# A two-model decoder kernel: retention, dilated and memory keys and the PLE rows turned by VectorE and a trip over DRAM

## The chip, the cores and the metric

The kernel is one program on one core of a Trainium2 chip. The metric is device time in microseconds (us) of one launch; lower is better. Of the kernel before, three runs are shown. Beside them stands one profiled execution, from which all durations of single instructions, waits and transfers are taken. Engine names are those of the profile: PE is TensorE's matmul stream, PEld its weight loads, DVE VectorE, ACT ScalarE, POOL GpSimd, SP the SyncE queue that issues all DMAs.

## The reference

Two stacks run one after the other on the same 256 x 1024 activations. Everything is float32.

```
first_block, 2 layers:
  mix   = hybrid_mixer(x)              # convolution + sparse attention + chunk attention, then w_mix_out
  x     = layer_norm(ALPHA*x + mix)
  k, v  = split(mem @ w_mkv)           # 256 memory rows, 4 heads of 256  -> "memory keys"
  cross = softmax(q k^T / 16) v @ w_mo ;  x = layer_norm(ALPHA*x + cross)
  x     = layer_norm(ALPHA*x + relu(x @ w1)^2 @ w2)
second_block, 4 layers (i = 0..3):
  a = rmsnorm(h)
  i = 0, 3: retention                  # q, k roped, 4 heads of 256; (q k^T * decay) v; silu(g) * y @ w_out
  i = 1   : dilated attention          # 3 groups x 16 heads of 64, windows 128/512/2048, dilations 1/4/16
  i = 2   : gated MLP with a token mix
  h = h + rmsnorm(mix) ;  h = h + rmsnorm(swiglu(rmsnorm(h)))
  emb  = p[i] @ ple_w_proj[i]          # 256 rows of 256: the "PLE rows"
  h    = h + sigmoid(rmsnorm(h) @ ple_w_gate[i]) * emb
```

## The kernel before

The 256 rows are two tiles of 128, and each tile t is worked by a Python generator, `thread(t)`. All weights form one list of blocks, mostly 128 x 1024 elements (512 KB), in the order of use. For each block n the main loop issues the loads up to `LOAD_AHEAD` = 6 blocks ahead (`load`, L199), splits the next block into a high and a low part (`split`: high on ACT at L225 or L284, low on DVE at L228 or L232), then lets thread 0 use block n and thread 1 use block n - lag, where the lag is 1 to 5 by stage (`LAGS`; 4 for the retention's "rq" and "rk", 1 for "dq", "dk", "dv", 5 for "pg"). Loaded blocks have 5 raw buffers, split parts 14. The order in which each engine gets its instructions is then set at build time by a scheduler over this program.

Each projection (`proj`) takes four blocks. Per block and thread it issues six 128x512 matmuls (high x high, high x low, low x high for two slices of the contraction, L326) into one of two banks "pj", which both threads share, and then calls `flush(t)`. `flush` runs what was put off: closures in `later[t]`, entries of `due[t]` that are counted down by one at each flush, and one step of a generator in `behind[t]` (attention that runs beside the projections).

A matmul contracts over partitions, so queries, keys and hidden rows have to be turned before they are used. There are two ways to do that in the kernel:

- `transpose4` (L279): up to four 128x128 blocks pass through TensorE against the identity matrix into one PSUM bank, and ACT or DVE copies the bank to SBUF. Retention queries and keys ("rqp", copied by ACT at L920), dilated queries and keys ("dqp", "dkp", copied by DVE at L1044), memory keys ("mkp", copied by DVE at L815) and PLE rows ("prp", cut by ACT at L284 and DVE at L315) go this way.
- `turn_by_dma`: DVE transposes 32x32 squares of the row block into a tile "xt" (L360, one instruction), four DMAs write it to a DRAM tile "xd" (L364, 64 KB each), one DMA reads it back turned into the source's own buffer (L367, `BACK` = 1 flush later), and `CUT` = 3 flushes later ACT and DVE cut it into high and low parts (L378, L379). Only the hidden rows of the feed-forward, retention and gated-MLP outputs go this way. "xt" comes from two buffers tagged "ET", which both threads share with the turned softmax rows of the attention.

The stages in order of time, by rows of the trace: the first block's last hidden row is squared at 850 us (L375); retention i = 0 copies its first query at 865 us (L905); the dilated scores run from 1313 to 1570 us (L979); the gated MLP's outputs are turned from 1872 to 1936 us (L360); the second retention copies its last key at 2228 us (L920); the last PLE rows are turned at 2566 us. The end of each layer of the second block is `embedding`: it loads the PLE rows, turns and cuts them and multiplies them with two blocks ("pep"), between the norm and the gate projection of the same thread.

Of the kernel before, what the change touches and what calls it, by code (L numbers as in the profile page):

```python
# [8 lines left out]
F32 = mybir.dt.float32  # L9
# [6 lines left out]
P = 128  # L16
# [14 lines left out]
DEFER = (1, 1, 1, 1, 1, 1, 1, 1)  # L31
# [17 lines left out]
def kernel(  # L49
# [7 lines left out]
    nc = tc.nc  # L57
# [294 lines left out]
        else:  # L352
            fn()

    def turn_by_dma(t, src, nkk, parts, j, square=None):


        w = 32 * nkk
        xt = sb.tile([P, 512], F32, tag=ETB[0].format(t=t), name="xt", bufs=ETB[1])[:, :4 * w]
        V.transpose(xt.rearrange("p (q k a) -> p q k a", q=4, a=32), src.rearrange("p (k q a) -> p q k a", q=4, a=32))  # L360
        d_ = dr.tile([4, 32, 4, P], F32, tag=f"xd{t}", name="xd")
        dv = d_.rearrange("q a i e -> (q a i e)")[0:P * 4 * w].rearrange("(q a i e) -> q a i e", q=4, a=32, i=4)
        for i in range(4):
            nc.sync.dma_start(dv[:, :, i, :].rearrange("q a e -> a q e"),  # L364
                              xt[32 * i:32 * i + 32, :].rearrange("a (q e) -> a q e", q=4))
        z = src
        due[t].append([BACK, lambda: nc.sync.dma_start(z, dv.rearrange("q a i e -> (q a) (i e)"))])  # L367

        def fin():
            bank = parts.banks[j] = newbank(t)  # L370
            zv = z.rearrange("p (i k b) -> p k i b", i=4, k=nkk)
            hi, lo = (x[:, 0:nkk, :].rearrange("p k (i b) -> p k i b", i=4) for x in bank)
            if square:
                f = sb.tile([P, 4, P], F32, tag=f"tq{t}", name="ffT", bufs=2)
                S.activation(f[:, 0:nkk, :].rearrange("p k (i b) -> p k i b", i=4), zv, AF.Square, scale=square)  # L375
                cut(bank, slice(0, nkk), f[:, 0:nkk, :])
            else:
                S.copy(hi, zv)  # L378
                V.tensor_tensor(out=lo, in0=zv, in1=hi.bitcast(F32), op=ALU.subtract)  # L379

        due[t].append([CUT, fin])
        due[t].sort(key=lambda d: d[0])

    def proj(t, xT, key, n, kind="pj"):
        p = bank(kind, t, [P, 512], "pj")
# [418 lines left out]
    def memory_block(t, l, j):  # L804

        own = slice(t * P, (t + 1) * P)
        p = yield from proj(t, memT[t], ("mkv", l, j), 512)
        if j < 2:
            r_ = sb.tile([P, 512], F32, tag=f"rB{t}", name="mk", bufs=2)
            S.copy(r_, p)  # L810
            kT = get2(("mkT", l, j), [P, 4, 256], "kv", 4)

            def turn():
                pt = transpose4(t, [r_[:, i * P:(i + 1) * P] for i in range(4)], "mkp")
                V.tensor_copy(kT[:, :, own], pt)  # L815

            defer(t, DEFER[7], turn)
        else:
            vv = get2(("mv", l, t), [P, D], "kv", 4)
            S.copy(vv[:, 512 * (j - 2):512 * (j - 1)], p)  # L820
# [6 lines left out]
    def cross(t, l, xT):  # L827
        qT = []
        oT = Parts()
        for j in range(2):  # L830
            p = yield from proj(t, xT, ("mq", l, j), 512)
            q = sb.tile([P, 512], F32, tag=f"rA{t}", name="mqr", bufs=2)
            if j:
                V.tensor_scalar(out=q, in0=p, scalar1=0.0625, scalar2=None, op0=ALU.mult)
            else:
                S.mul(q, p, 0.0625)
            pt = transpose4(t, [q[:, i * P:(i + 1) * P] for i in range(4)], "mqp")
            qT.append(sb.tile([P, 4, P], F32, tag=f"tq{t}", name="mqT", bufs=2))
            copy("s" if j else "v", qT[j], pt)
        for b in range(2):  # L840
            kT = shared[("mkT", l, b)]
            sp = bank("at", t, [P, 2, 256], "msp")
            for i in range(2):
                for c in range(2):
                    T.matmul(sp[:, i, :], qT[b][:, 2 * i + c, :], kT[:, 2 * i + c, :],
                             start=(c == 0), stop=(c == 1))
            pt, et, ev = turn_bank(t, softmax_bank(t, sp, 2, 2), 2)
            copy("v", et, pt)
            o = pt
            for i in range(2):  # L850
                for c in range(2):
                    c0 = 512 * b + 256 * i + 128 * c
                    for kt in range(2):
                        T.matmul(o[:, 2 * i + c, :], shared[("mv", l, kt)][:, c0:c0 + P], ev[:, i, kt, :],
                                 start=(kt == 0), stop=(kt == 1))
            oT.banks.append(newbank(t))
            cut(oT.banks[b], slice(0, 4), o, IALPHA)
        acc = newacc(t)
        yield from outproj(t, acc, ("mo", l), 8, oT, 0, True, True, xT)
        return acc  # L860
# [21 lines left out]
    def retention(t, i, hT, rs):  # L882
# [11 lines left out]
        hr = scaled(t, rs, 0.5, "hr")  # L894
        cbx = rcos[:, t:t + 1, :].to_broadcast([P, 4, P])
        sbx = rsin[:, t:t + 1, :].to_broadcast([P, 4, P])
        qT = [sb.tile([P, 4, P], F32, tag=f"tq{t}", name="rqT", bufs=2) for _ in range(2)]
        for nm in ("rq", "rk"):
            for j in range(2):
                p = yield from proj(t, hT, (nm, i, j), 512)  # L900
# [12 lines left out]
                bv = b.rearrange("p (h c) f -> p h c f", c=2)  # L913
                V.tensor_tensor(out=xv[:, :, 0, :], in0=xv[:, :, 0, :], in1=bv[:, :, 1, :], op=ALU.subtract)
                V.tensor_tensor(out=xv[:, :, 1, :], in0=xv[:, :, 1, :], in1=bv[:, :, 0, :], op=ALU.add)
                dst = qT[j] if nm == "rq" else get2(("rkT", i, j), [P, 4, 256], "kv", 4)[:, :, own]

                def turn(xs=xs, dst=dst):
                    pt = transpose4(t, [xs[:, k, :] for k in range(4)], "rqp")
                    S.copy(dst, pt)  # L920

                defer(t, DEFER[4], turn)
        acc = newacc(t)
        oT = Parts()
        for h in range(5):
            if h < 4:
# [6 lines left out]
                for c in range(nt):  # L933
                    kt = t - c
                    for d in range(2):
                        T.matmul(sp[:, c, :], kT[:, 2 * (h % 2) + d, kt * P:(kt + 1) * P], qT[h // 2][:, 2 * (h % 2) + d, :],  # L936
                                 start=(d == 0), stop=(d == 1))
                sm_ = sb.tile([P, 2, P], F32, tag=f"sc{t}", name="rsm")
                V.tensor_tensor(out=sm_[:, 0, :], in0=sp[:, 0, :], in1=rmask[:, h, :], op=ALU.mult)
                if t:  # L940
# [23 lines left out]
    def dilated(t, hT, rs):  # L964
# [6 lines left out]
        def attend(BT, qT, kT, vv, us, mx, sm_):  # L971
            firsts = [0, 1] if t == 0 else [0, 1, 4, 5]
            for b0 in range(0, len(firsts), 2):
                sps = [bank("at", t, [P, 512], "dsp").rearrange("p (h k) -> p h k", h=hpb) for _ in range(2)]
                for i in range(hpb):
                    for b in range(2):
                        h = firsts[b0 + b] + 2 * i
                        r = 64 * (h % 2)
                        T.matmul(sps[b][:, i, :], qT[r:r + 64, h // 2, :], kT[r:r + 64, h // 2, :nk],  # L979
                                 start=True, stop=True)  # L980
                sls = [slice(h0, h0 + 2 * hpb - 1, 2) for h0 in firsts[b0:b0 + 2]]
                es = []
                for b in range(2):
# [48 lines left out]
        for hf in range(2):  # L1032
# [3 lines left out]
            for g in range(3):  # L1036
                p = yield from proj(t, hT, ("dq", hf, g), 512)
                r_ = sb.tile([P, 512], F32, tag=f"rA{t}", name="dqr", bufs=2)
                S.activation(r_, p, AF.Copy, scale=sq[:, 0:1])
                qT = sb.tile([P, 4, P], F32, tag=f"tq{t}", name="ddqT", bufs=2)  # L1040

                def turn(r_=r_, dst=qT, nm="dqp"):
                    pt = transpose4(t, [r_[:, k * P:(k + 1) * P] for k in range(4)], nm)
                    V.tensor_copy(dst, pt)  # L1044

                defer(t, DEFER[5], turn)
                p = yield from proj(t, hT, ("dk", hf, g), 512)
                r_ = sb.tile([P, 512], F32, tag=f"rB{t}", name="dkr", bufs=2)
                S.activation(r_, p, AF.Copy, scale=rs[:, 0:1])
                kT = get2(("ddkT", hf, g), [P, 4, 256], "kv", 4)  # L1050
                defer(t, DEFER[5], lambda r_=r_, dst=kT[:, :, own], turn=turn: turn(r_, dst, "dkp"))
                p = yield from proj(t, hT, ("dv", hf, g), 512)
                vv = get2(("ddv", hf, g), [P, 2, 512], "kv", 4)
                S.activation(vv[:, t, :], p, AF.Copy, scale=rs[:, 0:1])
                us = sb.tile([P, 8, 64], F32, tag=f"U{t}", name="dUs", bufs=3)
                U.append(us)
                behind[t].append(attend(tiles[("db", hf, g)], qT, kT, vv, us, mall[:, g, :], sall[:, g, :]))
# [62 lines left out]
    def swiglu(t, i, hT, rs):  # L1120
# [2 lines left out]
        V.tensor_tensor(out=sc, in0=rs, in1=hr, op=ALU.mult)  # L1123
        acc = newacc(t)
        fT = Parts()
        for j in range(7):
            if j < 6:
                n = FG[j][1]
                nkk = n // P
# [11 lines left out]
        return acc  # L1141

    def embedding(t, i):
        pr = sb.tile([P, 256], F32, tag=f"sc{t}", name="pr")
        nc.sync.dma_start(pr, p2[i, t * P:(t + 1) * P, :])
        pt = transpose4(t, [pr[:, 0:P], pr[:, P:2 * P]], "prp")
        pT = Parts()
        pT.banks.append(newbank(t))
        cut(pT.banks[0], slice(0, 2), pt[:, 0:2, :])
        pp = [bank("pj", t, [P, 512], "pep") for _ in range(2)]  # L1150
        yield from outproj(t, pp, ("pp", i), 2, pT, 0, True, True)
        e = []
# [176 lines left out]
```

## Time and profile before

| what | value |
|---|---|
| runs | 2593.28, 2594.84, 2595.04 us; median 2594.84 us |
| profiled execution | 2594.81 us, span 2593.1 us, mean granted clock 0.998 |
| busy, share of the span | PE 98%, PEld 80%, DVE 70%, ACT 58%, POOL 2% |
| DMA | 500.97 MB, mean 193 GB/s, 62.7% of 16 engines on the SP queue |
| HBM | read 471.33 MB, written 27.26 MB |

The span runs from the first to the last instruction of the profiled execution; its time has 1.7 us more. A busy share is the share of the span in which an engine had an instruction running. Matmuls are pipelined, so the cost of one in a dense stream is read from the distance between starts in the timeline, not from its duration (a 128x512 matmul lasts 390 to 400 ns and starts every 0.23 us).

### The profile page before, as it was taken

To read this page: it belongs to the slowest core of one execution; us is meant where nothing else is said; L and a number is where in the kernel's file an instruction comes from. 1 tells how busy PE (TensorE), PEld (TensorE's weight loads), DVE (VectorE), ACT (ScalarE), POOL (GpSimd) and SP (SyncE) were. 2 spreads that over 40 slices of the span, in tenths; PEclk is the share of its full clock that TensorE was granted. 3 is DMA by queue.
4 is the path that set the end of the run, shared out by engine and by line. 5 is a ranking of instruction groups with operands and counts; after the bars stand their busy time and mean duration, and the time that the engine had idled before them with its cause. 6 is when DMAs were issued, how large, how long until landed. Compare 5 with 4: busy or idle time off the path is not lost. (4 is left out here: it accounts for less than half of the span.)

```text
span 2593.1 us, 36098 instructions
## 1 busy us (share of the span) xinstructions
PE 2546.9 (98%) x12308; PEld 2079.4 (80%) x12308; DVE 1815.5 (70%) x3333; ACT 1509.7 (58%) x2852; POOL 58.6 (2%) x88
## 2 busy tenths in 40 slices
PE   8999999999999999999999999999999999999998
PEld 7788788887788778788787878887877887887887
DVE  8865667866666866766766767667867677766766
ACT  6653555654455665555766666557656566655555
POOL 0000000000000000000000000000100000000000
PEclk9999999999999999999999999999999999999999
DMA  6453776554578566676654555766586775666764
GB/s 214 157 171 106 224 241 188 155 175 143 170 233 243 175 201 218 206 226 211 211 161 142 162 162 159 228 204 215 166 263 208 220 226 177 198 205 190 230 201 146
DMA packets 280904, 500.97 MB, mean 193 GB/s; under 512 B 28816, under 2 KB 101648, under 8 KB 279568
## 3 DMA queue, kind: packets, MB, share of 16 engines
q1 hardware_dynamic: 280720, 498.68, 62.7%
q8 instruction: 96, 1.57, 0.3%
q14 instruction: 88, 0.72, 0.1%
HBM read 471.33 MB, written 27.26 MB: 192 GB/s over the span
## 5 line engine op out<-in xcount | busy, mean ns | idle before, releaser
L326 PE MATMUL pj<-wh,part 128*128 128x512 f32 (+3 forms) x4480 | 1426.6, 385 | 2.5 <-ACT part L284 1.4
L326 PEld LDWEIGHTS pj<-wh,part 128*128 128x128 f32 x4480 | 832.3, 188 | 168.0 <-issue 9.4
L326 PE MATMUL pj<-wl,part 128*128 128x512 f32 (+3 forms) x2240 | 853.1, 381 | 1.3 <-DVE wl L228 1.3
L326 PE MATMUL acc<-wh,part 128*128 128x512 f32 x1920 | 582.7, 396 | 13.1 <-ACT part L284 6.3
L326 PEld LDWEIGHTS pj<-wl,part 128*128 128x128 f32 x2240 | 422.5, 189 | 77.0 <-issue 2.6
L326 PEld LDWEIGHTS acc<-wh,part 128*128 128x128 f32 x1920 | 358.0, 189 | 93.1 <-ACT part L284 8.4
L326 PE MATMUL acc<-wl,part 128*128 128x512 f32 x960 | 308.5, 394 | 0.1
L232 DVE TENSOR_TENSOR wl<-ff,wh 128x512 fp32r<-128x512 f32 x256 | 169.8, 686 | 104.2 <-ACT wh L284 104.2
L284 ACT CAST wh<-ff 128x512 fp32r<-128x512 f32 x256 | 152.8, 620 | 134.6 <-PE acc L326 65.3
L326 PEld LDWEIGHTS acc<-wl,part 128*128 128x128 f32 x960 | 181.5, 189 | 38.6 <-DVE wl L232 0.4
L225 ACT ACTIVATE wh<-fg,ngc 128x512 fp32r<-128x512 f32 (+1 forms) x192 | 126.5, 686 | 120.6 <-PE pj L326 64.1
L228 DVE SCALAR_TENSOR_TENSOR wl<-fg,ngc,wh 128x512 fp32r<-128x512 f32 (+1 forms) x192 | 129.5, 701 | 80.5 <-ACT wh L225 80.4
L228 DVE SCALAR_TENSOR_TENSOR wl<-fu,ngc,wh 128x512 fp32r<-128x512 f32 (+1 forms) x192 | 128.1, 704 | 51.8 <-ACT wh L225 48.6
L225 ACT ACTIVATE wh<-fu,ngc 128x512 fp32r<-128x512 f32 (+1 forms) x192 | 123.8, 684 | 59.8 <-PE acc L326 35.7
L284 ACT CAST wh<-fo 128x512 fp32r<-128x512 f32 x176 | 103.6, 621 | 78.0 <-PE pj L326 76.4
L232 DVE TENSOR_TENSOR wl<-fo,wh 128x512 fp32r<-128x512 f32 x176 | 115.0, 684 | 44.7 <-ACT wh L284 41.9
L225 ACT ACTIVATE wh<-rv,ngc 128x512 fp32r<-128x512 f32 x64 | 45.2, 722 | 40.9 <-PE pj L326 33.6
L232 DVE TENSOR_TENSOR wl<-ro,wh 128x512 fp32r<-128x512 f32 x64 | 43.4, 688 | 29.3 <-ACT wh L284 29.3
L228 DVE SCALAR_TENSOR_TENSOR wl<-rv,ngc,wh 128x512 fp32r<-128x512 f32 x64 | 46.8, 747 | 24.5 <-ACT wh L225 24.3
L228 DVE SCALAR_TENSOR_TENSOR wl<-pg,ngc,wh 128x512 fp32r<-128x512 f32 x64 | 46.5, 747 | 20.6 <-ACT wh L225 20.1
L232 DVE TENSOR_TENSOR wl<-mkv,wh 128x512 fp32r<-128x512 f32 x64 | 41.9, 686 | 26.7 <-ACT wh L284 26.5
L284 ACT CAST wh<-ro 128x512 fp32r<-128x512 f32 x64 | 39.3, 620 | 36.1 <-PE pj L326 28.6
(323 smaller groups left out, 3214.1 us busy)
## 6 DMA issues: line engine op xcount, KB each, us to landing
ff<-in_w_ff_dram SPq DMA_DIRECT2D x128, 512.0 KB, 4.3
fo<-in_ffn_out_dram SPq DMA_DIRECT2D x88, 512.0 KB, 4.4
fg<-in_ffn_in_dram SPq DMA_DIRECT2D x80, 512.0 KB, 4.5
fu<-in_ffn_in_dram SPq DMA_DIRECT2D x80, 512.0 KB, 4.1
xd<-xt SPq DMA_DIRECT2D x384, 64.0 KB, 2.4
mkv<-in_w_mkv_dram SPq DMA_DIRECT2D x32, 512.0 KB, 4.0
rv<-in_ret_in_dram SPq DMA_DIRECT2D x32, 512.0 KB, 4.5
rg<-in_ret_in_dram SPq DMA_DIRECT2D x32, 512.0 KB, 3.8
```

What stands on the lines that cost most here:

```text
L225: S.activation(h_, r_, AF.Copy, scale=gc)
L228: V.scalar_tensor_tensor(out=l_, in0=r_, scalar=gc, in1=h_.bitcast(F32), op0=ALU.mult, op1=ALU.subtract)
L232: (V if le == "v" else G).tensor_tensor(out=l_, in0=r_, in1=h_.bitcast(F32), op=ALU.subtract)
L284: S.copy(o, i)
L326: T.matmul(outs[i], a, ws[i][b], start=s0, stop=s1)
```

## The change

Four kinds of rows leave `transpose4`. Two helpers are cut out of `turn_by_dma`: `trip` (the 32x32 transposes and the four DMAs out) and `put_off` (an entry in `due`). A new helper `turn_to` uses them. If the destination can take the order in which the rows come back, the DMA writes straight into it; otherwise the DMA comes back into the source and ACT copies from there with the columns put in order.

The key tiles, and the retention's query tile, get an order of columns with 32 tokens of one feature slice in a row, so that DMA can write them: memory keys `[P, 8, 4, 32]`, dilated keys `[P, 8, 4, 32]`, retention queries `[P, 4, 4, 32]`. The score matmuls read them as 8 or 4 runs of 32 elements. Retention keys (`[P, 2, 4, P]`) and dilated queries keep whole columns and take the copy on ACT. The PLE rows are loaded at step j = 3 of the feed-forward, sent on the trip at j = 4 and cut 21 flushes later; `embedding` only picks them up.

```
+    def trip(t, src, nkk):
         w = 32 * nkk
...      # xt, V.transpose, xd and the four DMAs out as before
+        return dv.rearrange("q a i e -> (q a) (i e)")
+
+    def put_off(t, n, f):
+        due[t].append([n, f])
+        due[t].sort(key=lambda d: d[0])
+
+    def turn_to(t, src, nkk, dst):
+        back = trip(t, src, nkk)
+        if len(dst.shape) == 3:
+            put_off(t, BACK, lambda: nc.sync.dma_start(src, back))
+            put_off(t, CUT, lambda: S.copy(dst.rearrange("p k (i b) -> p k i b", b=32),
+                                           src.rearrange("p (i k b) -> p k i b", i=4, b=32)))
+        else:
+            put_off(t, BACK, lambda: nc.sync.dma_start(dst.rearrange("p i k b -> p (i k b)"), back))
+
+    def turn_by_dma(t, src, nkk, parts, j, square=None, at=CUT):
+        back = trip(t, src, nkk)
         z = src
+        put_off(t, BACK, lambda: nc.sync.dma_start(z, back))
...
+        put_off(t, at, fin)
...  memory_block
-            kT = get2(("mkT", l, j), [P, 4, 256], "kv", 4)
-            def turn():
-                pt = transpose4(t, [r_[:, i * P:(i + 1) * P] for i in range(4)], "mkp")
-                V.tensor_copy(kT[:, :, own], pt)
-            defer(t, DEFER[7], turn)
+            kT = get2(("mkT", l, j), [P, 8, 4, 32], "kv", 4)
+            turn_to(t, r_, 4, kT[:, 4 * t:4 * t + 4])
...  cross
-                    T.matmul(sp[:, i, :], qT[b][:, 2 * i + c, :], kT[:, 2 * i + c, :],
+                    T.matmul(sp[:, i, :].rearrange("p (i b) -> p i b", b=32), qT[b][:, 2 * i + c, :], kT[:, :, 2 * i + c, :],
...  retention
-        qT = [sb.tile([P, 4, P], F32, tag=f"tq{t}", name="rqT", bufs=2) for _ in range(2)]
+        qT = [sb.tile([P, 4, 4, 32], F32, tag=f"tq{t}", name="rqT", bufs=2) for _ in range(2)]
...
-                dst = qT[j] if nm == "rq" else get2(("rkT", i, j), [P, 4, 256], "kv", 4)[:, :, own]
-                def turn(xs=xs, dst=dst):
-                    pt = transpose4(t, [xs[:, k, :] for k in range(4)], "rqp")
-                    S.copy(dst, pt)
-                defer(t, DEFER[4], turn)
+                turn_to(t, xf, 4, qT[j] if nm == "rq" else get2(("rkT", i, j), [P, 2, 4, P], "kv", 4)[:, t])
...
-                        T.matmul(sp[:, c, :], kT[:, 2 * (h % 2) + d, kt * P:(kt + 1) * P], qT[h // 2][:, 2 * (h % 2) + d, :],
-                                 start=(d == 0), stop=(d == 1))
+                        f = 2 * (h % 2) + d
+                        T.matmul(sp[:, c, :].rearrange("p (i b) -> p i b", b=32), kT[:, kt, f, :],
+                                 qT[h // 2][:, :, f, :], start=(d == 0), stop=(d == 1))
...  dilated
-                        T.matmul(sps[b][:, i, :], qT[r:r + 64, h // 2, :], kT[r:r + 64, h // 2, :nk],
-                                 start=True, stop=True)
+                        T.matmul(sps[b][:, i, :].rearrange("p (i b) -> p i b", b=32), qT[r:r + 64, h // 2, :],
+                                 kT[r:r + 64, 0:4 * nkt, h // 2, :], start=True, stop=True)
...
-                def turn(r_=r_, dst=qT, nm="dqp"):
-                    pt = transpose4(t, [r_[:, k * P:(k + 1) * P] for k in range(4)], nm)
-                    V.tensor_copy(dst, pt)
-                defer(t, DEFER[5], turn)
+                turn_to(t, r_, 4, qT)
...
-                kT = get2(("ddkT", hf, g), [P, 4, 256], "kv", 4)
-                defer(t, DEFER[5], lambda r_=r_, dst=kT[:, :, own], turn=turn: turn(r_, dst, "dkp"))
+                kT = get2(("ddkT", hf, g), [P, 8, 4, 32], "kv", 4)
+                turn_to(t, r_, 4, kT[:, 4 * t:4 * t + 4])
...  swiglu
+        pT = shared[("pT", i, t)] = Parts()
+        pT.banks.append(None)
         for j in range(7):
+            if j == 3:
+                pr = sb.tile([P, 256], F32, tag=f"sc{t}", name="pr")
+                nc.sync.dma_start(pr, p2[i, t * P:(t + 1) * P, :])
+            if j == 4:
+                turn_by_dma(t, pr, 2, pT, 0, at=21)
...  embedding
-        pr = sb.tile([P, 256], F32, tag=f"sc{t}", name="pr")
-        nc.sync.dma_start(pr, p2[i, t * P:(t + 1) * P, :])
-        pt = transpose4(t, [pr[:, 0:P], pr[:, P:2 * P]], "prp")
-        pT = Parts()
-        pT.banks.append(newbank(t))
-        cut(pT.banks[0], slice(0, 2), pt[:, 0:2, :])
+        pT = shared.pop(("pT", i, t))
```

More of the change, by code (lines that the diff above doesn't have):

```diff
@@ L353, in defer @@
             fn()
-    def turn_by_dma(t, src, nkk, parts, j, square=None):
+    def trip(t, src, nkk):
         w = 32 * nkk
@@ L365, in turn_by_dma @@
                               xt[32 * i:32 * i + 32, :].rearrange("a (q e) -> a q e", q=4))
+        return dv.rearrange("q a i e -> (q a) (i e)")
[12 more added lines that the diff above has]
+        back = trip(t, src, nkk)
         z = src
-        due[t].append([BACK, lambda: nc.sync.dma_start(z, dv.rearrange("q a i e -> (q a) (i e)"))])
+        put_off(t, BACK, lambda: nc.sync.dma_start(z, back))
         def fin():
@@ L379, in fin @@
                 V.tensor_tensor(out=lo, in0=zv, in1=hi.bitcast(F32), op=ALU.subtract)
-        due[t].append([CUT, fin])
-        due[t].sort(key=lambda d: d[0])
+        put_off(t, at, fin)
     def proj(t, xT, key, n, kind="pj"):
```

## The prediction

> **What bounds the kernel now.** I read the busy shares first, then TensorE's waits, then groups, timeline and stages.
>
> ```profile
> span 2593.1 us, 36098 instructions
> ...
> PE 2546.9 (98%) x12308; PEld 2079.4 (80%) x12308; DVE 1815.5 (70%) x3333; ACT 1509.7 (58%) x2852; POOL 58.6 (2%) x88
> ```
>
> TensorE is idle for only 2593.1 - 2546.9 = 46.2 us. Whatever leaves its stream leaves the span, as long as the others keep up. Its waits (total, times, longest):
>
> ```profile
> PE acc L326 <- ACT part L378: 4.5, 3, 1.7
> PE pep L326 <- ACT part L284: 4.2, 4, 1.0
> PE prp L279 <- DVE part L315: 3.1, 4, 0.8
> ```
>
> The last two belong to the change: four of the eight PLE transposes wait for a PSUM bank, and the blocks behind them wait for the cut.
>
> **The removed transposes.** Groups by tile (busy us, mean ns):
>
> ```profile
> L279 PE MATMUL rqp<-tab,rxs 128*128 128x128 f32 x64 | 12.2, 277 | 0.4
> L279 PE MATMUL dkp<-tab,dkr 128*128 128x128 f32 x48 | 7.2, 272 | 0.0
> L279 PE MATMUL dqp<-tab,dqr 128*128 128x128 f32 x48 | 7.2, 272 | 0.0
> L279 PE MATMUL mkp<-tab,mk 128*128 128x128 f32 x32 | 4.8, 272 | 0.0
> L279 PE MATMUL prp<-tab,pr 128*128 128x128 f32 x16 | 3.4, 291 | 3.1 <-DVE part L315 3.1
> ```
>
> So 16 + 24 + 8 = 48 groups of four, and 8 pairs. Busy times overlap the neighbours, so the price is read from starts in the timeline:
>
> ```profile
> 1289.39 0.39 PE L326 MATMUL pj<-wh,part 128*128 128x512 f32 x1
> 1289.62 0.60 PE L279 MATMUL dqp<-tab,dqr 128*128 128x128 f32 x4
> 1289.98 0.48 PE L326 MATMUL pj<-wh,part 128*128 128x512 f32 x1
> 1290.29 0.40 PE L326 MATMUL pj<-wl,part 128*128 128x512 f32 x1
> ```
>
> From 1289.39 to 1290.29 is 0.90 us. Two 512-column matmuls at the usual 0.23 us take 0.46, so a group costs 0.44 us. 48 x 0.44 = 21.1 us. A pair is taken as half a group: 8 x 0.22 = 1.8 us.
>
> **The PLE wait.** The PLE rows are loaded, turned and cut during the feed-forward, so "pep" can start as soon as TensorE reaches it: 3.1 + 4.2 = 7.3 us of idle go. What is late next is the norm's own cut, which the gate projection needs; the "pep" blocks and the other thread's "acc" blocks lie ahead of it, so I give it nothing here and a rival below. The same stretch shows a slower clock (stretches; the column before the DMA share is the granted clock):
>
> ```profile
> core 0: us, PE busy (x) PEld busy (x) DVE busy (x) ACT busy (x) POOL busy (x), PEclk, DMA share, GB/s
> 1242.00:1245.40 3.40, 1.57 (x7) 0.95 (x7) 3.40 (x9) 2.68 (x7) 0.93 (x1) 1.00 0.70 216
> 1773.00:1776.40 3.40, 1.79 (x8) 1.29 (x9) 3.40 (x8) 2.30 (x6) 0.93 (x1) 0.99 0.71 233
> 1776.00:1779.00 3.00, 3.00 (x10) 2.38 (x9) 0.88 (x2) 0.00 (x0) 0.00 (x0) 0.55 0.69 239
> 2554.20:2557.20 3.00, 3.00 (x9) 2.33 (x9) 1.57 (x4) 0.00 (x0) 0.00 (x0) 0.56 0.67 199
> ```
>
> Twice, just after this wait, TensorE runs 3 us at 0.55 or 0.56, losing some 1.4 us in each; with the edges I take 1.6 us, 3.2 us in all. After the wait at 1242 us the clock stays at 1.00 in its row although TensorE was no busier. The ends are 0 (slow stretches come again elsewhere) and 3.2; I take 3.2, since the idle beside which both rows stand is what goes.
>
> The Trainium skill (TensorE: Matmul & The Clock Gate, Part 1, the HAM clock gate) says that a free-running window of about 3.4 us with little activity halves the clock until a busy window has passed. By that rule the phase of the window decides which gap is punished: the sum would be anywhere from 0 to 3.2 us by it, and 3.2 by the rows; the row at 1242 us, idle without a slow stretch, speaks for the rule.
>
> Gross: 21.1 + 1.8 + 7.3 + 3.2 = 33.4 us.
>
> **What VectorE and ScalarE take over.**
>
> ```profile
> L360 DVE STREAM_TRANSPOSE xt<-ffu 128x512 f32<-128x512 f32 x40 | 28.3, 708 | 0.7
> ...
> L1044 DVE COPY ddqT<-dqp 128x512 f32<-128x512 f32 x12 | 8.3, 688 | 6.9 <-PE dqp L279 6.9
> L1044 DVE COPY ddkT<-dkp 128x512 f32<-128x512 f32 x12 | 8.2, 687 | 1.6 <-PE dkp L279 1.6
> ```
>
> ```profile
> L815 DVE COPY mkT<-mkp x8: 679/688/692, 117.5 to 557.2; 128x512 f32<-128x512 f32 x8
> ```
>
> ```profile
> L920 ACT COPY rqT<-rqp x8: 565/578/589, 874.8 to 2208.7; 128x512 f32<-128x512 f32 x8
> L920 ACT COPY rkT<-rqp x8: 565/568/574, 894.7 to 2228.2; 128x512 f32<-128x512 f32 x8
> ```
>
> For dilated rows and memory keys a DVE copy of 0.69 us becomes a DVE transpose of 0.71 us: 32 of each, nothing net. In the retention the copies are on ACT, so DVE gains 16 x 0.71 = 11.3 us, eight in each of two stages; the eight half-width PLE transposes add under 0.5 us each during feed-forwards. ACT loses 8 copies for the retention queries and gains 12 for the dilated queries (0.57 us each): 2 us, at 58% busy. What DVE has to spare in these stages:
>
> ```profile
> 868.00:912.00 44.00, 42.45 (x199) 33.04 (x198) 37.80 (x68) 31.32 (x54) 1.00 (x1) 1.00 0.59 186
> 2196.00:2240.00 44.00, 43.79 (x208) 35.67 (x208) 33.17 (x56) 29.21 (x46) 0.00 (x0) 1.00 0.64 202
> 100.00:130.00 30.00, 29.87 (x166) 23.81 (x166) 26.48 (x64) 19.08 (x45) 0.11 (x1) 1.00 0.63 204
> ```
>
> First retention: TensorE's 44 us lose 8 x 0.44 = 3.5, to 40.5; DVE goes from 37.8 to 37.8 + 5.7 = 43.5. DVE would be the bound by 3.0 us. The following blocks can lend nothing for sure, since splits run little ahead, so I charge all of it. Second: 33.2 + 5.7 = 38.9, below 40.5: nothing. Memory keys: TensorE gives 4 x 0.44 = 1.8 of 30 us, DVE stays at 26.5: nothing. Ends: 0 and 7.0 (neither retention gains). I take 3.0.
>
> **The trips.** Each of 48 trips adds four DMAs of 64 KB out and one of 256 KB back, each of the 8 PLE trips half of that: 280 issues. Bytes: 52 x 512 KB = 27 MB on 501. KB each, median us to landing:
>
> ```profile
> xd<-xt SPq DMA_DIRECT2D x384, 64.0 KB, 2.4
> ...
> ffu<-xd SPq DMA_DIRECT2D x40, 256.0 KB, 4.6
> ```
>
> ```profile
> L364 SPq DMA_DIRECT2D xd<-xt x416: 303/432/1906, 258.6 to 2545.0; - x139
> ```
>
> ```profile
> SPq L199 <- DVE wl L228: 851.4, 362, 9.4
> ```
>
> 280 issues at up to 0.43 us are 120 us of SP, which spends 851 us waiting for freed load buffers alone: hidden, and a blocked SP has these to give before a weight is late. A trip takes 0.7 + 4 x 0.43 + 2.4 + 4.6 = 9.4 us and up. Its reader comes four or five blocks later at the least (dilated keys, first retention key), at 6 matmuls x 2 threads x 0.23 = 2.8 us a block and more with attention: 11 to 18 us. Covered; if the cover went, each late trip would cost what it is late. In the retention two trips go with four loads of 512 KB: 3.1 MB in 10.1 us, 311 GB/s. What the DMA engines do in dense stretches:
>
> ```profile
> 2112.00:2134.00 22.00, 22.00 (x131) 19.47 (x130) 17.52 (x33) 15.24 (x32) 0.47 (x1) 1.00 0.88 270
> ```
>
> ```profile
> 873.00:884.00 11.00, 10.97 (x54) 8.44 (x53) 10.05 (x21) 9.15 (x18) 1.00 (x1) 1.00 0.79 287
> ```
>
> Scaled to a full share, 307 with trips and 363 with loads alone. So the retention's keys and queries run at the DMA engines' edge; at 307 the 12.6 MB of 40.5 us take 41.0. Ends 0 and 4 us (both stages late by 2); I take 1.0.
>
> **The copies that wait for landings.** Twenty ACT copies (8 retention keys, 12 dilated queries) stand in ACT's order behind a DMA, ahead of weight splits and of the projections' evacuations. The trips that exist show the price:
>
> ```profile
> ACT part L378 <- DMA ffu<-xd: 26.0, 28, 1.8
> ACT ffT L375 <- DMA ffr<-xd: 20.8, 26, 1.6
> ACT part L378 <- DMA ro<-xd: 18.4, 12, 3.0
> ```
>
> 65.2 us in 66 waits, about 1.0 us each, of which 4.5 us reached TensorE (the first row of its waits). 20 x 4.5 / 66 = 1.4 us; I take 1.0, since the reader is farther off here. Ends 0 and 20.
>
> **Reading in runs of 32.** 96 + 192 + 64 = 352 score matmuls read one operand in runs of 32 elements. No TensorE row shows that; ACT reads the same order at L378 as fast as whole rows at L284:
>
> ```profile
> L378 ACT CAST part<-ffu x48: 401/620/623, 1086.6 to 2553.8; 128x512 fp32r<-128x512 f32 x40, 128x256 fp32r<-128x256 f32 x8
> ```
>
> ```profile
> L284 ACT CAST wh<-ff x256: 600/622/625, 238.3 to 839.1; 128x512 fp32r<-128x512 f32 x128
> ```
>
> I take 0; it cannot gain, since the columns are the same; the upper end is below.
>
> **Sum.** 33.4 - 3.0 - 1.0 - 1.0 = 28.4 us off the profiled 2594.81 us, which is the median of the runs (2594.84): **2566 us**, -1.1%.
>
> **Rivals.**
>
> VectorE or the DMAs hold the retentions and the memory keys, and only dilated rows and PLE pay: 24 x 0.44 + 1.8 + 7.3 + 3.2 = 22.9, less 2.0: 2574 us. For it: 37.8 of 44 us busy. Against: the second retention at 33.2.
>
> The PLE wait comes back as a wait of the gate projection for the norm's cut: 28.4 - 10.5 = 17.9 us, 2577 us. For it: DVE is busy for all 3.40 us at 1242 and 1773 us. Against: four matmul blocks lie between.
>
> Slower: ACT's waits on landings reach TensorE through the two shared "pj" banks. Place: the 20 copies in retention and dilated attention; decisive at 28.4 / 20 = 1.4 us more for each. If each keeps TensorE as long as the longest wait above, 3.0 us, 60 us are lost against 29 gained: 2626 us. For it: DMA at its edge in the retention; against: 65.2 us of such waits cost 4.5.
>
> Slower too: the runs of 32 cost TensorE time. The score rows:
>
> ```profile
> L845 PE MATMUL msp<-mkT,mqT 128*128 128x256 f32 x64 | 16.4, 379 | 0.0
> ```
>
> At 0.26 us each, the 352 would have to slow by 28.4 / 352 = 0.08 us, a third, to cancel the gain; doubled, 2595 - 28 + 90 = 2657 at the most. Only ACT's row speaks against it.
>
> Slower by the engine: the work goes from TensorE (0.44 us a group) to DVE (0.71 us) and the DMAs. Were splits on DVE the bound all along, DVE's net 11.3 + 3.5 us would be added: 2610 us. Against: DVE 70%, and 98% on TensorE.
>
> The Trainium skill (VectorE: DVE Perf Modes, Rules for kernel authors) says to transpose 128x128 on TensorE where PSUM may be the destination, and that DVE does 32x32 squares only. By that rule the old way is the better one, which is the case just priced; no row shows TensorE waiting for it.
>
> **Chances.** Forecast, 2558 to 2573: 0.58. Below 2558 (all of the gross and some other idle): 0.05. First rival 0.12, second 0.10. Within 0.2%, about what a measurement can tell, gains eaten by several of these: 0.05. Slower: landings 0.05, runs 0.03, engine 0.02. So faster 0.85, same 0.05, slower 0.10; the range 2557 to 2588 leaves out the slower cases, the unchanged one and the extreme gain. Its upper end is about 22 of the 28 us lost.
>
> **What will show it.** TensorE busy down by about 22 us, idle by about 5; no "rqp", "dkp", "mkp", "prp"; 280 more DMA issues; DVE above 95% and TensorE waiting for "wl" near 870 to 912 us for the first charge; no stretch near 0.55 clock at the embeddings; score matmuls at the old 0.26 us. It is wrong if "rsp" or "dsp" wait for "xd" landings, if "pj" waits for ACT, or if those matmuls last longer.

## The result, and the profile after

The changed kernel takes 2569.31 us (median of four, 2566.06 to 2570.4) against 2594.94 us of the kernel before, run in turn with it on the same chip: ratio 0.9896 [0.9881, 0.9910]. In a second comparison on another chip it took 2564.73 us, ratio 0.9890 [0.9877, 0.9903]. The forecast was 2566 us. Below, a difference in us is one minus the ratio, times the time before: 27.0 us in the first comparison and 28.5 us in the second, against 28.4 forecast. The total came right; two of its terms did not, and they offset each other.

The page of the changed kernel, its span and its busy shares (profiled execution 2566.06 us):

```profile
span 2564.3 us, 36170 instructions
...
PE 2521.9 (98%) x12100; PEld 2059.6 (80%) x12100; DVE 1823.3 (71%) x3357; ACT 1501.9 (59%) x2856; POOL 60.0 (2%) x88
```

TensorE has 208 instructions less, the 64 + 48 + 48 + 32 + 16 transposes, and is busy 25.0 us less (forecast about 22). Idle went from 46.2 to 42.4 us (forecast about 5 less). Of TensorE's waits (total, times, longest) these are new or had a counterpart before:

```profile
PE acc L326 <- ACT part L397: 4.9, 4, 1.4
...
PE pj L326 <- DVE wl L228: 1.3, 1, 1.3
PE pj L326 <- DVE part L315: 1.1, 1, 1.1
PE pj L326 <- ACT embh L1161: 1.0, 5, 0.2
```

"pep" and "prp" wait no more. The rows "pj" for "part L315" and for "embh" are new. "embh" is ACT's work on the embedding, behind which the gate projection's bank comes free: 1.0 us of the 7.3 us came back there. "part L315" is one wait, at 869 us, where VectorE's cut for the first retention's projections comes 1.1 us late. The wait for landings, L378 before and L397 now, is 4.9 us where it was 4.5, and the wait for "wl" is 1.3 us as it was before.

Where the time went is read from the starts of the 10,080 projection and output matmuls ("pj", "acc", "pep"), all of L326, which both traces have in the same number: the k-th start before, minus the k-th start after.

| stage (time before) | part | forecast | measured |
|---|---|---|---|
| to 845 us | memory keys | 3.5 | 3.0 |
| 845 to 1200 and 2160 to 2540 us | retention | 7.0 - 3.0 - 1.0 | 3.6 + 4.7 |
| 1260 to 1700 us | dilated attention | 10.6 | 5.7 |
| the four ends of layers | PLE rows | 1.8 + 7.3 + 3.2 | 2.6 + 3.7 + 2.3 + 3.5 = 12.1 |
| everywhere | copies on ACT | -1.0 | no row of its own |

These are single traces. A boundary that moves by a few us shifts a row by up to 0.4 us, and the first row, 3.0 us here, is 1.3 us in e0_after and 6.3 us in e5_pairs, whose first blocks are the same. The two ends of layers with 3.7 and 3.5 us are those where the kernel before had a stretch at half speed.

The two retentions and the two embeddings, stretches (us, then busy time of PE, PEld, DVE, ACT and POOL, then the granted clock, the DMA share and GB/s):

```profile
858.00:902.00 44.00, 41.62 (x186) 33.59 (x185) 41.85 (x79) 25.06 (x44) 1.66 (x3) 1.00 0.70 216
2168.00:2212.00 44.00, 44.00 (x197) 36.48 (x196) 35.82 (x63) 24.97 (x41) 0.00 (x0) 1.00 0.75 224
1242.00:1245.40 3.40, 3.26 (x16) 2.40 (x15) 3.34 (x7) 2.75 (x8) 0.55 (x1) 1.00 0.70 202
1772.00:1775.00 3.00, 3.00 (x14) 2.34 (x14) 2.83 (x5) 2.66 (x5) 0.00 (x0) 1.00 0.61 182
```

In the first retention DVE is busy for 41.85 of 44 us, a little more than TensorE, and still no "wl" wait of TensorE lies there; the one wait of 1.1 us is all that it shows for it. At 1772 us, where TensorE had been idle, it is now busy throughout at full clock.

The copies on ACT that wait for landings (all instructions of their line):

```profile
L377 ACT COPY ddqT<-dqr x12: 602/605/622, 1288.4 to 1527.7; 128x512 f32<-128x512 f32 x12
...
L377 ACT COPY rkT<-rxs x8: 602/607/619, 901.2 to 2217.7; 128x512 f32<-128x512 f32 x8
its engine sat idle before it (us, times) until:
  DMA dqr<-xd: 0.2, 1
```

Twenty copies waited 0.2 us in all for their data: the trips are back in time.

The score matmuls (groups by shape: busy us, mean ns, idle before). Before:

```profile
L979 PE MATMUL dsp<-ddkT,ddqT 64*128 64x256 f32 x96 | 19.2, 410 | 0.0
```

After:

```profile
L987 PE MATMUL dsp<-ddkT,ddqT 64*128 64x256 f32 x96 | 23.3, 415 | 0.0
L858 PE MATMUL msp<-mkT,mqT 128*128 128x256 f32 x64 | 16.5, 380 | 0.0
L944 PE MATMUL rsp<-rqT,rkT 128*128 128x128 f32 x96 | 13.3, 274 | 0.0
```

"msp" stands where it was (16.4 us) although it now reads runs of 32. The dilated scores of thread 1 have 4.1 us more. The timeline shows why (start, length, instruction, how many in a row). Before, all eight instructions of four scores are in a row in 6 of 12 groups; five more are cut once, into two and six, and one into four pieces:

```profile
1383.03 1.14 PE L979 MATMUL dsp<-ddkT,ddqT 64*128 64x256 f32 x8
1415.47 0.70 PE L979 MATMUL dsp<-ddkT,ddqT 64*128 64x256 f32 x2
1416.47 1.13 PE L979 MATMUL dsp<-ddkT,ddqT 64*128 64x256 f32 x6
```

After, again six are in a row, but the other six are cut apart further by transposes of the other thread's softmax rows, five into four pieces and one into three:

```profile
1356.40 0.70 PE L987 MATMUL dsp<-ddkT,ddqT 64*128 64x256 f32 x2
1357.03 0.44 PE L279 MATMUL ptp<-tab,ss 128*128 128x128 f32 x2
1357.40 0.70 PE L987 MATMUL dsp<-ddkT,ddqT 64*128 64x256 f32 x2
1358.02 0.33 PE L279 MATMUL ptp<-tab,ss 128*128 128x128 f32 x1
1358.28 0.70 PE L987 MATMUL dsp<-ddkT,ddqT 64*128 64x256 f32 x2
```

A score of thread 1 is two instructions on 64 of 128 partitions. Alone it keeps TensorE from 1356.40 to 1357.03 us, 0.63 us. Two scores on the lower and the upper 64 partitions that follow each other run side by side: the group of eight at 1383.03 us has its starts in twos 7 ns apart, and the next matmul starts 1.07 us after its first, where four scores alone take 2.5 us. Summed from start to start, the 96 instructions took 17.8 us before and 21.3 us after, and the stage's 144 softmax transposes "ptp" 15.4 and 16.6 us: 3.5 + 1.2 = 4.7 us, nearly the 10.6 - 5.7 = 4.9 us that the stage is short. The 96 transposes of queries and keys, 8.7 us from start to start, and the matmuls beside them, which take 1.8 us less, make up 10.4 us: the stage gained what was forecast and lost 4.7 us of it to the order.

### The profile page after: what moved, and what is told of

The parts are those of the page before. It is cut to its first block, busy times and chain, and to the rows that moved or that the text cites. A ratio compares the mean times of both kernels' runs of the same rounds, so it can differ in the third digit from the quotient of the medians.

```text
span 2564.3 us, 36170 instructions
## 1 busy us (share of the span) xinstructions
PE 2521.9 (98%) x12100; PEld 2059.6 (80%) x12100; DVE 1823.3 (71%) x3357; ACT 1501.9 (59%) x2856; POOL 60.0 (2%) x88
## 5 line engine op out<-in xcount | busy, mean ns | idle before, releaser
L326 PE MATMUL pj<-wh,part 128*128 128x512 f32 (+3 forms) x4480 | 1415.4, 384 | 4.9 <-ACT part L284 1.4
L326 PEld LDWEIGHTS pj<-wh,part 128*128 128x128 f32 x4480 | 831.2, 188 | 174.3 <-issue 8.9
L326 PE MATMUL pj<-wl,part 128*128 128x512 f32 (+3 forms) x2240 | 852.9, 381 | 1.3 <-DVE wl L228 1.3
L326 PE MATMUL acc<-wh,part 128*128 128x512 f32 x1920 | 582.2, 395 | 12.8 <-ACT part L284 5.9
L326 PEld LDWEIGHTS pj<-wl,part 128*128 128x128 f32 x2240 | 421.9, 188 | 79.1 <-DVE wl L228 2.7
L326 PEld LDWEIGHTS acc<-wh,part 128*128 128x128 f32 x1920 | 356.8, 189 | 92.5 <-ACT part L284 8.4
L326 PE MATMUL acc<-wl,part 128*128 128x512 f32 x960 | 307.1, 393 | 0.1
L326 PEld LDWEIGHTS acc<-wl,part 128*128 128x128 f32 x960 | 180.8, 188 | 38.3 <-DVE wl L232 0.6
L228 DVE SCALAR_TENSOR_TENSOR wl<-rg,ngc,wh 128x512 fp32r<-128x512 f32 x64 | 44.9, 748 | 19.7 <-ACT wh L225 19.6
L284 ACT CAST wh<-mkv 128x512 fp32r<-128x512 f32 x64 | 37.5, 620 | 36.2 <-PE acc L326 21.2
L228 DVE SCALAR_TENSOR_TENSOR wl<-pg,ngc,wh 128x512 fp32r<-128x512 f32 x64 | 46.3, 748 | 15.9 <-ACT wh L225 15.4
```

What stands on the lines that cost most here:

```text
L228: V.scalar_tensor_tensor(out=l_, in0=r_, scalar=gc, in1=h_.bitcast(F32), op0=ALU.mult, op1=ALU.subtract)
L284: S.copy(o, i)
L326: T.matmul(outs[i], a, ws[i][b], start=s0, stop=s1)
```

## The experiments

The theory: the price of a group, 0.44 us, and the PLE term hold; most of the charge on the retention is not paid, because VectorE's full window hardly stalls TensorE; the dilated attention lost to the new order of its scores. The rivals: the parts help each other, so that no part alone says what it is worth; runs of 32 slow the dilated scores; VectorE has become the bound.

**Each part alone, on the kernel before.** e1_ple:

```
     for j in range(7):
+        if j == 3:
+            pr = sb.tile([P, 256], F32, tag=f"sc{t}", name="pr")
+            nc.sync.dma_start(pr, p2[i, t * P:(t + 1) * P, :])
+        if j == 4:
+            turn_by_dma(t, pr, 2, pT, 0, at=21)
...
-    pt = transpose4(t, [pr[:, 0:P], pr[:, P:2 * P]], "prp")
```

> The kernel before with the PLE part alone: rows loaded and sent on the trip during the feed-forward, cut before the embedding. Stream theory with the wait: 1.8 us of transposes and 7.3 us of idle go, and up to 3.2 us of half clock beside it: 9 to 12.5 us faster, 2582 to 2586 us; the two waits at 'prp' and 'pep' gone. Rival (the wait comes back as a wait of the gate projection for the norm's cut): 2 us faster, 2593 us, with about 7 us of 'pj' waiting for 'part'.

2582.97 us, ratio 0.9955 [0.9942, 0.9967]: 11.7 us. The PLE term holds alone.

e2_dil:

```
-                defer(t, DEFER[5], turn)
+                turn_to(t, r_, 4, qT)
...
+                kT = get2(("ddkT", hf, g), [P, 8, 4, 32], "kv", 4)
+                turn_to(t, r_, 4, kT[:, 4 * t:4 * t + 4])
```

> The kernel before with the dilated queries and keys alone. By the prediction's sum: 10.6 us faster, 2584 us. By the two traces, in which the dilated stage gave only 5.8 us: 5 to 6.5 us faster, 2589 us, and the 256-column score matmuls 'dsp' again at a sum of about 21.3 us between starts instead of 17.8, broken into twos by softmax turns 'ptp'. If the shortfall came from the other parts of the change (a busier DMA or ScalarE), this part alone gives the 10.6.

2592.91 us, ratio 0.9998 [0.9987, 1.0008]: nothing, although 24 groups of transposes are gone. Its groups by shape, and a stretch at the stage's end:

```profile
L997 PE MATMUL dsp<-ddkT,ddqT 64*128 64x256 f32 x96 | 24.4, 427 | 0.0
```

```profile
1553.00:1563.00 10.00, 10.00 (x34) 7.49 (x34) 5.30 (x13) 5.49 (x18) 1.10 (x1) 0.55 0.48 157
```

The scores are cut apart as in the changed kernel (22 times two, six times eight, once four), and in this profiled execution TensorE then runs 10 us at a clock of 0.55. By the k-th starts the lead of 4.6 us at 1550 us is gone behind that stretch. It does not explain the other runs: the mean clocks of all eleven average 0.9975, against 0.9979 for the kernel before, which is about 1 us. The expectation of 5 to 6.5 us is missed, and why this part gives nothing alone, but 5.7 us inside the changed kernel's trace, stays open.

e3_ret, the retention's `turn_to` alone:

```
-                defer(t, DEFER[4], turn)
+                turn_to(t, xf, 4, qT[j] if nm == "rq" else get2(("rkT", i, j), [P, 2, 4, P], "kv", 4)[:, t])
```

> The kernel before with the retention queries and keys alone. Stream theory without a charge: 16 groups of 0.44 us, 7.0 us faster, 2588 us. The prediction's theory (VectorE the bound in the first retention, DMA engines at their edge): 2.0 to 4.0 us faster, 2592 us, with TensorE waiting for 'wl' near 870 to 912 us. VectorE busy in that window is expected at 95% or more under both.

2585.48 us, ratio 0.9967 [0.9954, 0.9979]: 8.6 us where the prediction gave 3.0 for both stages. The first retention as a stretch, and TensorE's waits from 862 to 960 us:

```profile
862.00:906.00 44.00, 41.64 (x185) 33.56 (x184) 41.79 (x79) 25.17 (x44) 1.68 (x3) 1.00 0.68 212
```

```profile
PE pj L326 <- DVE part L315: 1.1, 1, 1.1
PE pj L326 <- ACT part L284: 0.7, 1, 0.7
PE xTp L279 <- DVE x L553: 0.6, 1, 0.6
```

DVE at 95% of the window, no wait for "wl", and again the one of 1.1 us for "part".

e4_mem, the memory keys' `turn_to` alone:

```
-            defer(t, DEFER[7], turn)
+            kT = get2(("mkT", l, j), [P, 8, 4, 32], "kv", 4)
+            turn_to(t, r_, 4, kT[:, 4 * t:4 * t + 4])
```

> The kernel before with the memory keys alone. Stream theory: 8 groups of 0.44 us, 3.5 us faster, 2591.4 us. Rival (VectorE at 96% at 110 to 126 us is the bound there): under 1.8 us faster, 2593 us.

2590.97 us, ratio 0.9985 [0.9977, 0.9994]: 3.9 us, with 3.5 forecast. The four parts alone sum to 24.7 us, 27.0 to 28.5 together. Each of these differences is good to some 3 us, so the sums agree; part by part the dilated one does not (0.5 us alone).

**Again, as a base for the next ones.** e0_after is the changed kernel, unaltered.

> The changed kernel again, on the chip of the three below. 2569 us; runs spread over some 4 us if the half-clock stretches come and go between executions. Its granted clock in each run should then fall as its time rises, by about 0.0007 for each 1.7 us.

2564.73 us, ratio 0.9890 [0.9877, 0.9903], 4 us less than expected. The slowest of its four runs (2568.22 us) has the lowest mean clock, 0.997; the others have 0.998 and 0.999.

**The PLE rows early, but still by TensorE** (e6_early, on the kernel before): load at j = 3, transposes and cut during the feed-forward.

```
+                def early(pr=pr):
+                    pt = transpose4(t, [pr[:, 0:P], pr[:, P:2 * P]], "prp")
+                    pT.banks[0] = newbank(t)
+                    cut(pT.banks[0], slice(0, 2), pt[:, 0:2, :])
+                due[t].append([21, early])
```

> The kernel before with the PLE rows still turned by TensorE, but loaded at step 3 and turned and cut at the 21st flush after step 4 of the feed-forward: no trip over DRAM, no work taken from TensorE. If the PLE part's gain is the wait and its slow clock: 7 to 10.5 us faster, 2585 to 2588 us, nearly all of what the PLE part gives. If it were the transposes: under 2 us faster, 2593 us.

2584.95 us, ratio 0.9967 [0.9955, 0.9979]: 8.6 of the 11.7 us come from turning the rows earlier; the trip itself adds 3.1 us, where 1.8 was forecast for the eight pairs (both times are good to some 3 us). TensorE's waits from 1200 to 1260 us, where the first of them stood, are now

```profile
PE acc L326 <- ACT part L378: 0.2, 1, 0.2
```

**Is VectorE the bound in the retention?** e8_twice turns each retention row block twice, 16 x 0.71 = 11.3 us more on DVE, in the changed kernel.

```
-        V.transpose(xt.rearrange(...), src.rearrange(...))
+        for _ in range(2 if twice else 1):
+            V.transpose(xt.rearrange(...), src.rearrange(...))
```

> The changed kernel with each 32x32 transpose of the retention's queries and keys done twice into the same tile: 16 x 0.71 = 11.3 us more of VectorE, half in each retention, nothing else. If VectorE bounds the first retention already: 5.7 us slower for it and 2 to 5 us for the second, 2577 to 2580 us. If VectorE still has slack where it looks full, because its lead over TensorE is drawn down: 0 to 3 us slower, 2569 to 2572 us.

2567.52 us (2564.6 to 2575.72), ratio 0.9903 [0.9889, 0.9917]: 3 us over e0_after by the medians, with intervals that overlap. Both retentions as stretches, and TensorE's waits from 840 to 960 us:

```profile
862.00:906.00 44.00, 41.02 (x170) 32.65 (x169) 40.76 (x74) 24.01 (x41) 0.99 (x1) 0.92 0.67 204
2160.00:2204.00 44.00, 43.98 (x195) 35.52 (x194) 43.04 (x80) 27.69 (x47) 0.92 (x1) 1.00 0.71 214
```

```profile
PE acc L326 <- ACT part L284: 2.9, 1, 2.9
PE xTp L279 <- DVE x L554: 2.3, 2, 1.7
PE pj L326 <- ACT part L284: 0.7, 1, 0.7
PE pj L326 <- DVE rth L955: 0.4, 1, 0.4
```

DVE's busy time rose by 9.1 us only (1822.8 in e0_after, 1831.9 here), since a transpose lasts 0.71 us but DVE starts its next instruction 0.63 us after it. With DVE at 43.04 of 44 us in the second retention (40.20 in the same window of the changed kernel) TensorE is busy for 43.98. A VectorE that bound TensorE would have cost the 9 us. By the medians about 3 us show; the intervals alone would allow up to 10, but the traces show less. In the first retention e8_twice has 7 us at half speed, which is the 0.92 of its row and costs 3.4 us, and e0_after has half of that. With this set aside, the two retentions come some 2 us later than in either trace of the changed kernel (an estimate from the k-th starts). The waits for DVE in the second view are 2.7 us, where the changed kernel has 1.7 us from 855 to 960 us (1.1 for "part" and 0.6 for "x", as e3_ret).

**Order or runs of 32?** e5_pairs keeps the changed kernel's layout and adds to the build-time order, with no wait on the chip, that thread 1's first score of a group comes behind thread 0's last softmax transpose.

```
+            last_turn[t] = T.transpose(p[:, i, :], s, ident)
...
+                        m_ = T.matmul(sps[b][:, i, :]..., start=True, stop=True)
+                        if t and i == 0 and b == 0:
+                            tc.add_manual_dep(m_.ins, last_turn[0].ins.name, NoSync)
```

> The changed kernel with one order fixed at build time: the 256-column dilated scores of thread 1 are issued behind the softmax turns of thread 0, so that each group of eight stays together and two 64-row matmuls run side by side. Theory (the dilated stage lost 4.8 us to the order on TensorE): 'dsp' back to about 17 us between starts, 3.5 to 5 us faster than the changed kernel, 2565 us. Rival (reading in runs of 32 slows the 64-row scores): 'dsp' stays at 21 us, time unchanged at 2569 us.

2565.56 us, ratio 0.9890 [0.9877, 0.9902]: the same as the changed kernel. The scores did what was hoped:

```profile
L989 PE MATMUL dsp<-ddkT,ddqT 64*128 64x256 f32 x96 | 14.1, 402 | 0.0
```

All 12 groups are whole; from start to start they take 13.3 us, against 17.8 before and 21.3 after. So runs of 32 cost nothing, and the order was the cause. But the time is given back at the end of the stage, where no projection is left to stand beside the last group. Stretch, and TensorE's waits from 1525 to 1585 us:

```profile
1525.00:1560.00 35.00, 31.65 (x174) 23.56 (x173) 22.95 (x47) 15.32 (x49) 1.10 (x1) 0.97 0.46 158
```

```profile
PE ptp L1013 <- ACT ET L286: 1.2, 2, 0.7
PE ptp L281 <- ACT ss L513: 1.2, 2, 0.8
PE dop L281 <- DVE dUs L1039: 0.5, 1, 0.5
```

TensorE has nothing between the two threads' softmaxes there. The lead over the kernel before falls from 24.6 us at 1550 us to 19.2 us at 1580 us: 3.3 us of idle, and 1.7 us in a stretch at half speed at 1558 us.

**The order for all but the last group** (e9_pinned): as e5_pairs, and the edge is left out where nothing covers it.

```
-                        if t and i == 0 and b == 0:
+                        if pin and t and i == 0 and b == 0:      # pin: (hf, g) != (1, 2)
```

> The changed kernel with the order fixed as in the pairs kernel, but not for the last group of the second half, whose attention runs with no projections left to cover it. The pairs kernel had 'dsp' at 13.3 us between starts instead of 21.3, and lost it again in that stretch by 3.3 us of idle and a half-clock stretch. Theory (the order is worth about 6 us where projections cover it): 'dsp' near 14 us, no idle of over 1 us between 1520 and 1570 us, 4 to 7 us faster than the changed kernel, 2558 to 2562 us. Rival (the time goes elsewhere whatever the order): 2565 us or more.

2557.42 us (2552.34 to 2559.05), ratio 0.9851 [0.9837, 0.9865], 38.7 us: the best of all, below both kernels. Page, group and the stage's end:

```profile
span 2555.0 us, 36177 instructions
...
PE 2514.9 (98%) x12100; PEld 2057.0 (81%) x12100; DVE 1822.3 (71%) x3357; ACT 1499.5 (59%) x2856; POOL 59.7 (2%) x88
```

```profile
L989 PE MATMUL dsp<-ddkT,ddqT 64*128 64x256 f32 x96 | 15.1, 404 | 0.0
```

```profile
1520.00:1570.00 50.00, 49.31 (x266) 39.52 (x265) 39.22 (x75) 31.54 (x79) 2.33 (x3) 1.00 0.59 188
```

From 1260 to 1580 us the stage now gains 14.3 us (5.7 in the changed kernel), and TensorE is busy for 49.31 of 50 us at its end.

**What of that is the order alone?** e12_order is the kernel before with the same edge; e11_dilpin is e2_dil with it.

> The kernel before, turns on TensorE as they were, with the order alone fixed. 'dsp' from 17.8 us to about 13.5 us between starts: 3 to 5 us faster, 2590 us.

> The kernel before with the dilated queries and keys on the trip and the same order fixed. Theory (the trips give the 10.6 us once the order does not take it back, and the order adds some): 10 to 14 us faster than before, 2581 to 2585 us. Rival (trips in the dilated stage cost what they save, by ScalarE or the shared buffers): 4 to 5 us faster, what the order alone gives, 2590 us.

e12_order: 2590.62 us, ratio 0.9985 [0.9976, 0.9993], 3.9 us. e11_dilpin: 2582.24 us, ratio 0.9948 [0.9935, 0.9962], 13.5 us. In both, 11 of the 12 groups are whole. Their difference, 9.6 us, is what the dilated trips are worth when the order is the same on both sides; 24 x 0.44 = 10.6 was forecast. The intervals leave some 4 us either way; in the traces the stage (1260 to 1700 us) gains 13.8 and 3.2 us, which differ by 10.6.

**One more step on the same road** (e10_chunk): e9_pinned with the queries and keys of the first block's chunk attention on the trip too.

```
-        defer(t, DEFER[6], lambda: turn(cq, cqT, "cqp"))
+        turn_to(t, cq[:, 0:384], 3, cqT)
...
-        defer(t, DEFER[6], lambda: turn(ck, ckT[:, :, own], "ckp"))
+        turn_to(t, ck[:, 0:384], 3, ckT[:, :, own])
```

> The pinned kernel with the chunk attention's queries and keys (8 groups of three transposes) on the trip too. At 0.11 us a transpose 8 x 0.33 = 2.6 us and more at the switch: 2.5 to 3.5 us faster than the pinned kernel, 2556 to 2559 us. Rival: VectorE at 80 to 96% before 130 us bounds the first layer's half of it: 1 to 2 us.

2560.64 us, ratio 0.9867 [0.9854, 0.9881]: 3 us slower than e9_pinned by the medians, though 3.7 us of transposes are gone. TensorE's waits over the whole run:

```profile
PE acc L328 <- ACT part L286: 7.2, 5, 2.2
...
PE pj L328 <- ACT cq L751: 1.9, 1, 1.9
```

They are 5.2 and 0.4 us in e9_pinned. TensorE is busy as long as in e9_pinned (2514.8 and 2514.9 us) and idle for 43.3 us where it was 40.1. From start to start, the first block's scores "sp" and its "ptp" instructions also take 3.1 us more (14.3 to 15.8, 39.2 to 40.8). Of the cause only these rows are shown: waits for ACT and a new order once more; which of the two decides is open.

## Why the prediction was right, and where it was not

**The price of a group: right, but for the retention.** 0.44 us read from the starts in the timeline. Memory keys 3.0 to 3.9 us for 3.5; dilated 9.6 us for 10.6 once the order is held. Busy times would have given 0.65 us a group. The retention gave 8.6 us alone for 7.0 gross. Read by starts, its 16 groups took 9.1 us in the kernel before, 0.57 each, since TensorE came to six of them before DVE had the rows ready (the tile "rqp" before, what its engine waited for):

```profile
  DVE rxs L914: 2.3, 6
```

The prediction read one group of the dilated stage and carried its price over.

**The PLE wait: right in sum, 11.7 us alone for 12.3.** Of the wait 1.0 us returned in front of the gate projection ("embh"), not the 10.5 us of that rival (2577 us). e6_early puts three quarters on the wait and its slow clock. How much of it is clock can be bounded from all fourteen profiles. The six kernels that turn the PLE rows at the end of a layer have a stretch of 3.4 us at half speed at 12 of their 24 ends, as at three of the four in e12_order:

```profile
1770.20:1773.60 3.40, 3.37 (x8) 2.69 (x9) 1.88 (x4) 0.29 (x1) 0.00 (x0) 0.50 0.79 266
2135.40:2138.80 3.40, 3.40 (x10) 2.63 (x10) 0.83 (x2) 0.19 (x1) 0.00 (x0) 0.51 0.77 279
2551.80:2555.20 3.40, 3.40 (x10) 2.70 (x9) 1.37 (x4) 0.00 (x0) 0.00 (x0) 0.51 0.73 246
```

The eight profiles with the rows turned early, e6_early among them, which still turns them by TensorE, have none at their 32 ends. Two stretches an execution at 1.7 us each are 3.4 us, for 3.2 forecast; single executions of the old way have from one to three. So what stood at the ends of layers is gone. But some of it comes back elsewhere, as in e0_after, which has four stretches in other places: the mean clocks average 0.9977 over all 90 runs with the old turn, 0.9987 over the ten runs of e1_ple and e6_early, and 0.9981 over all 36 runs with the rows turned early, which is 2.6 us and 1.0 us gained. The term lies between the ends 0 and 3.2 us that the prediction gave, not at the upper one. The Trainium skill (TensorE: Matmul & The Clock Gate, Part 1) calls the window of the clock gate free-running. That 12 of 24 like waits were followed by a slow stretch agrees with it.

**The charge on the retention: the first term mis-sized.** "DVE would be the bound by 3.0 us", and 1.0 us for the DMA engines. Measured: 8.3 us in the trace and 8.6 us alone where 3.0 was left. The step compared DVE's busy time with TensorE's in one 44 us window and charged the excess as if DVE's work had to end with the window. It did not: DVE was at 41.85 us there, and what followed was one wait of 1.1 us for a cut, not 3.0 us for "wl"; twice the transposes on DVE (e8_twice) cost some 3 us by the medians, not 9 to 11. The size was off besides: a transpose keeps DVE for 0.63 us, not 0.71, and the gross term was 9.1 us, not 7.0. The copies on ACT were charged 1.0 us and waited 0.2 us.

**The dilated attention: the second term mis-sized, 10.6 us for 5.7.** The step took what leaves TensorE's stream as what leaves the span, with all else in its place. But the order of every engine is set at build time over the whole program; with 96 transposes gone the scheduler put the softmax turns of thread 0 between the scores of thread 1, and five of twelve groups went from two pieces to three or four: 4.7 us with the softmax transposes. Neither "will show it" nor a rival had this; the listed sign (score matmuls at their old duration) was watched for another cause, the runs of 32, which cost nothing.

**The sum** held because +5.3 us in the retention and -4.9 us in the dilated stage cancel. The total alone would have confirmed both wrong terms.

**The other rivals.** VectorE or DMA holding the retention (2574 us), ACT's landings (2626 us), runs of 32 (up to 2657 us) and VectorE as the bound (2610 us): each is spoken against by a row above. The rule that went with the last, to transpose 128x128 on TensorE (Trainium skill, VectorE: DVE Perf Modes, Rules for kernel authors), would have kept the 8.6 us of e6_early and left the rest of the 27.0 to 28.5 us, about 0.7%: the trip is the faster way in this kernel, with TensorE at 98% and VectorE at 71%.

## What to carry to other kernels

Price what leaves the bounding engine by distances between starts, not by busy times, in each stage where it stands, and then ask what the new build-time order does to the instructions that stay: compare, stage by stage, the k-th start of work that both versions share, since a right total can hide two wrong terms. A window in which an off-path engine is nearly full is no stall until a wait of the bounding engine names it. Matmuls on half the partitions are worth keeping adjacent, and an ordering edge that holds them together should be left off where no other work covers the wait that it makes.

## What the runs showed of the hardware that was not expected

- Scores on the lower and the upper 64 partitions ran side by side only when adjacent: eight instructions in 1.07 us, against 0.63 us for every two alone. Adjacency was not always enough: the last group of the stage is eight in a row (at 1569 us before) and took 1.58 us; the trace does not show why. The Trainium skill (TensorE: Matmul & The Clock Gate, Part 3) says that matmuls on different row groups overlap, with starts about 4 ns apart; the trace has 7 ns.
- An fp32 operand read in runs of 32 elements cost TensorE nothing here: 208 ns from start to start for "msp" and 97 ns for "rsp", before and after, and 1.06 us for an unbroken group of eight "dsp" in both.
- Half-speed stretches of TensorE come back at the same places, but not in every execution: at the ends of layers counted above, and between 842 and 875 us in 12 of the 14 profiles (before, TensorE waits 2.5 us there). The changed kernel has one in its first profile (near 848 us) and four in its second (two from 66 us, one each at 851 and 872 us). A stretch of 3.4 us loses 1.7 us, so a few of them are of the size of the 4 us by which runs of one kernel differ.
- A DVE busy for 43.04 of 44 us left TensorE busy for 43.98 of them (e8_twice, second retention).
